# Feed-forward blocks of a four-layer trunk: one of the two left-hand tiles that share a buffer starts 192 bytes later

## The chip, the cores and the metric

The kernel is written for Trainium2 and runs on one core of one chip. The metric is the time of one execution on the device in microseconds (us), and of several runs the median is compared. The engines are named as in the profile: PE is TensorE's matmul side and PEld its weight loads, DVE is VectorE, ACT ScalarE, POOL GpSimd, SP SyncE. SBUF is the on-chip memory with 128 partitions; a tile takes the same bytes of each partition, and an address below is a byte within a partition.

## The reference

A trunk of four layers over 512 rows of width 1024. Each layer adds a mixer (S5, gated linear attention (GLA), differential attention, S5 again) and then a feed-forward part:

```
def swiglu_ffn(h, w_gate_up, w_down):
    g, u = jnp.split(h @ w_gate_up, 2, axis=-1)
    return (jax.nn.silu(g) * u) @ w_down

for layer in range(DEPTH):
    h = rmsnorm(x, norm_mix[layer])
    ...
    x = x + mix.astype(x.dtype)
    h = rmsnorm(x, norm_ffn[layer])
    x = x + swiglu_ffn(h, ffn_w_gate_up[layer], ffn_w_down[layer]).astype(x.dtype)
return rmsnorm(x, norm_final)
```

The hidden width is 2816, and all data are 32-bit floats.

## The kernel before, in words

**Split numbers.** A 32-bit product is made of three matmuls in the float32r type. Each operand is kept as a high and a low part: ACT writes the high part (a cast, line 366 for weights), DVE the difference to it (line 374). The matmuls are high by high, high by low, low by high. A weight tile's pair is `whl`, of which there are five buffers of 8,192 bytes each.

**Blocks of the feed-forward part.** The hidden width is cut into 11 blocks of 256. A block's gate and up products are not eight products of quarters but seven, by a Strassen-like scheme: sums of quarters of the left side are multiplied by sums of quarters of the weights. `seven_product` (line 561) issues one such product as 24 matmuls: two halves `j` of the output, four pieces `k` of the inner width, three pairs of high and low. In each of them the weights (128x128, from `whl`) are the stationary operand and the left side (128x256) is the moving one. PE loads the weights of a matmul while an earlier one streams. From a block's number 2 on the order within the block is one, five, six, two, seven, three, four, so `one` is the first product and `two` the fourth. `one` accumulates into the bank `a`, `two` into the bank `d`. The names of their left sides are "11" and "12", and both lie in one tile, `sides`. The other five products take their left sides from tiles of their own: `side1` (five), `side2` (six), `side3` (seven), `side4` (three) and `side22` (four), in the profile all `side`. The first two blocks of each layer are interleaved by a written list of steps (`plan` in `ffn`); there the two `two` follow each other, then `five` and `six` of both, while ACT and DVE make the left sides `side1`, `side2` and so on, and the weights.

After each three or four blocks, `gemm_b` multiplies their results (`act`) with the down weights (lines 394 to 396, 512 columns at a time), and its last pieces write x.

**Who orders the work.** Within an engine the written order stands. Tiles come from pools with a fixed number of buffers; a pool's buffers lie side by side, and pools lie in the order in which they are opened: constants (`cp`), x (`xp`), left sides (`hp`, tag hT, two buffers), weights (`wp`), norms (`np_`), small statistics (`sp`), and behind them what each stage opens. So a pool that grows moves all that lies behind it. `Sides.room` takes the two buffers of tag hT for the tile of the four quarters (`halves`, F in the code) and for `sides`. `edge` takes some bytes only so that what follows begins later.

The start addresses, as the program is built, and what is left of them after division by 512:

| tile | start, before | rest | start, after | rest |
|---|---|---|---|---|
| `whl`, five buffers, 8,192 apart | 63,424 | 448 | 63,936 | 448 |
| "11", high part (in `sides`) | 30,656 or 47,040 | 448 | 30,144 or 47,040 | 448 |
| "12", high part (in `sides`) | 38,848 or 55,232 | 448 | 38,528 or 55,424 | 128 |
| `side1`, `side2` | 132,736, 140,928 | 128 | the same | 128 |
| `side4`, `side3`, `side22`, layers 1 and 2 | 149,120 and on | 128 | the same | 128 |
| `side4`, `side3`, `side22`, layers 0 and 3 | 194,432 and on | 384 | the same | 384 |
| `act` | 149,184 and on | 192 | the same | 192 |

A part's four pieces `k` lie 1,024 bytes apart, the low part of a left side and of a weight pair 4,096 behind its high part, and the second half `j` of a weight piece 512 behind the first. So the rest by 512 is the same for all 24 matmuls of a product.

**The small tiles.** `cos2` and `sin2` are the tables of the rotation in the attention layer; `diff_tables` writes them during layer 1's feed-forward part, `factors` reads them once. `pw` holds powers for the S5 layers and was last read in layer 0's feed-forward part. `ms` in GLA's `readout`, `st`, `sums` and `nm` in the attention are statistics from the pool `sp`, with eight buffers each where nothing else is said.

Of the kernel before, what the change touches and what calls it, by code (L numbers as in the profile page):

```python
# [11 lines left out]
F32 = mybir.dt.float32  # L12
F32R = mybir.dt.float32r
# [3 lines left out]
ALU = mybir.AluOpType  # L17
# [4 lines left out]
P = 128  # L22
# [45 lines left out]
class Left:  # L68
# [18 lines left out]
    def room(self):  # L87
        self.hT = [self.tr.hp.tile([P, KT, SEQ], F32R, tag="hT", name=f"hT{z}") for z in range(2)]
# [72 lines left out]
class Sides(Left):  # L161
# [11 lines left out]
        return xs  # L173

    def room(self):
        F = self.tr.hp.tile([P, 4, 4, 256], F32, tag="hT", name="halves")
        self.whole = F
        self.F = {(0, 0): F[:, 0], (1, 0): F[:, 1], (0, 1): F[:, 2], (1, 1): F[:, 3]}
        two = self.tr.hp.tile([P, 2, 2, 4, 256], F32R, tag="hT", name="sides")
        self.place = {"11": two[:, 0], "12": two[:, 1]}  # L180
        self.heads = []

    def quarter(self, q, half, b):
# [9 lines left out]
    def open(self, pool, names):  # L193

        for n in names:
            self.place[n] = pool.tile([P, 2, 4, 256], F32R, name="side" + n)

    def freed(self):

        return [self.F[k] for k in ((0, 0), (0, 1), (1, 0), (1, 1))]  # L200

    def parts(self, name, src, ks=slice(0, 4)):
        o = self.place[name][:, :, ks]
        self.tr.nc.scalar.copy(o[:, 0], src)
        self.tr.nc.vector.tensor_tensor(o[:, 1], src, o[:, 0].bitcast(F32), op=ALU.subtract)

    def keep(self, t, d, p):
        for j in range(4):
# [24 lines left out]

    def high(self, name):
        for ks, y in self.of(name):
            self.tr.nc.scalar.copy(self.place[name][:, 0, ks], y)

    def low(self, name):
        for ks, y in self.of(name):
            o = self.place[name][:, :, ks]  # L240
            self.tr.nc.vector.tensor_tensor(o[:, 1], y, o[:, 0].bitcast(F32), op=ALU.subtract)


class Chunks:
# [42 lines left out]
class Trunk:  # L287
# [263 lines left out]
    def seven_product(self, side, w, bank, first, hl=None):  # L551

        if hl is None:
            hl = self.halves(w, 4, 256)
        mm = self.nc.tensor.matmul
        for j in range(2):
            c = slice(j * P, (j + 1) * P)
            o = bank[:, j * 256 : (j + 1) * 256]
            for k in range(4):
                for n, (x, y) in enumerate(((0, 0), (0, 1), (1, 0))):  # L560
                    mm(  # L561
                        o, hl[:, x, k, c], side[:, y, k], start=first and not (j or k or n),
                        stop=k == 3 and n == 2, skip_group_check=True,
                    )

# [1287 lines left out]
    def gla(self, l, left):  # L1853
# [5 lines left out]
        with self.tc.tile_pool(name="gla", bufs=1) as p:  # L1859
# [112 lines left out]
            def readout(hf, t):  # L1972
                st, o_h = sts[hf], on[hf]
                oo = row(self.tp("op"))
                ms = self.sp.tile([P, 2], F32, tag="ms2", name="ms")
                for z in range(2):
                    h = 2 * hf + z
                    zs = slice(z * 256, (z + 1) * 256)
                    for c in range(2):
                        ch = 2 * t + c  # L1980
                        nc.tensor.matmul(
                            oo[c * 64 : (c + 1) * 64, zs], qT[:, h, ch * 64 : (ch + 1) * 64], st[z][:, ch],
                            start=True, stop=True,
                        )
                for z in range(2):
                    junk = T("e")
                    nc.scalar.activation(
                        junk[:, :256], oo[:, z * 256 : (z + 1) * 256], AF.Square, scale=1.0 / 16.0,
                        accum_out=ms[:, z : z + 1],
                    )  # L1990
                r_ = self.rsqrt(ms[:], 2, 1e-6)
                for z in range(2):
                    h = 2 * hf + z
                    zs = slice(z * 256, (z + 1) * 256)
                    v.scalar_tensor_tensor(
                        o_h[:, t, zs], oo[:, zs], r_[:, z : z + 1], ng[:, h * 256 : (h + 1) * 256],
                        op0=ALU.mult, op1=ALU.mult,
                    )
# [67 lines left out]
    def diff_tables(self):  # L2066
        nc, i = self.nc, self.i
        v = nc.vector
        cp = self.cp
        self.cos2 = cp.tile([P, NT, 16], F32, name="cos2")  # L2070
        self.sin2 = cp.tile([P, NT, 16], F32, name="sin2")
        self.cidq = cp.tile([P, NT], F32, name="cidq")
        self.neglam = cp.tile([P, 1], F32, name="neglam")
        yield
        p = Slices(self.wp.tile([P, 2048], F32, tag="whl", name="dtab", bufs=5))
        if True:
            pi = p.tile([NT, P], I32, name="pi")
            nc.sync.dma_start(pi[:], i["positions"][0].rearrange("(t p) -> t p", p=P))
            ci = p.tile([NT, P], I32, name="ci")
            v.tensor_scalar(ci[:], pi[:], 6, None, op0=ALU.arith_shift_right)  # L2080
            pf = p.tile([NT, 2, P], F32, name="pf")
            v.tensor_copy(pf[:, 0], pi[:])
            v.tensor_copy(pf[:, 1], ci[:])
            yield
            yield
            yield
            ps = self.tp("pps")
            for z in range(2):
                nc.tensor.transpose(ps[:, z, :NT], pf[:, z], self.ident[:NT, :NT])
            yield  # L2090
            yield
            pos = p.tile([P, NT], F32, name="pos")
            v.tensor_copy(pos[:], ps[:, 0, :NT])
            v.tensor_copy(self.cidq[:], ps[:, 1, :NT])
            ang = p.tile([P, NT, 8], F32, name="ang")
            freq = np.float32(500000.0) ** (-np.arange(8, dtype=np.float32) / np.float32(8))
            for j in range(8):
                v.tensor_scalar_mul(ang[:, :, j], pos[:], float(freq[j]))
            yield
            red = p.tile([P, 32], F32, name="red")  # L2100
            self.reduce_angle(p, red[:], ang[:].rearrange("p t j -> p (t j)"), 32, "r")
            sn = p.tile([P, NT, 8], F32, name="sn")
            cs = p.tile([P, NT, 8], F32, name="cs")
            fl = lambda x: x[:].rearrange("p t j -> p (t j)")
            yield
            self.sincos(p, fl(sn), fl(cs), red[:], 32, "r")
            yield
            yield
            for z in range(2):
                v.tensor_copy(self.cos2[:, :, z * 8 : z * 8 + 8], cs[:])  # L2110
            v.tensor_scalar_mul(self.sin2[:, :, 0:8], sn[:], -1.0)
            v.tensor_copy(self.sin2[:, :, 8:16], sn[:])
            yield
            lm = p.tile([P, 4, 64], F32, name="lm")
            for z, s in enumerate(("diff_lam_q1", "diff_lam_k1", "diff_lam_q2", "diff_lam_k2")):
                nc.sync.dma_start(lm[:, z], i[s][0].partition_broadcast(P))
            pr = p.tile([P, 2, 64], F32, name="pr")
            lv = lm[:].rearrange("p (a b) n -> p a b n", b=2)
            v.tensor_tensor(pr[:], lv[:, :, 0], lv[:, :, 1], op=ALU.mult)
            sm = p.tile([P, 2], F32, name="sm")  # L2120
            v.tensor_reduce(sm[:], pr[:], op=ALU.add, axis=AX.X)
            ex = p.tile([P, 2], F32, name="ex")
            yield
            self.exp(p, ex[:], sm[:], 2, "l")
            yield
            v.tensor_tensor(self.neglam[:], ex[:, 1:2], ex[:, 0:1], op=ALU.subtract)
            v.tensor_scalar_add(self.neglam[:], self.neglam[:], -LAMBDA_INIT)

    def diff(self, l, left):
# [4 lines left out]
        with self.tc.tile_pool(name="diff", bufs=1) as p:  # L2134
# [90 lines left out]
            def prepare(j):  # L2225
# [13 lines left out]
                        self.nc.gpsimd.dma_start(qs[to, m], hl[rows, z, 0])  # L2239
                        self.nc.gpsimd.dma_start(ks[to, m], hl[rows, :, 1])  # L2240
                ready[j] = qs, ks
                st = self.sp.tile([P, 2, NT], F32, tag="st", name="st")
                o_s = p.tile([P, NT, P], F32, tag="o_s", name="o_s", bufs=2)
                kept[j] = st, o_s

# [2 lines left out]
            def scores(i):  # L2248
# [1 line left out]
                ts = slice(t * P, (t + 1) * P)  # L2250
                qs, ks = ready[j]
                st = kept[j][0]
                pr, sums = [], self.sp.tile([P, 4], F32, tag="sums", name="sums")
                ss = [self.sbank("s"), self.sbank("s")]
                for m in range(2):
                    for z in range(2):
                        nc.tensor.matmul(ss[m][:], qs[:, m, ts], ks[:, m, z], start=z == 0, stop=z == 1)  # L2257
                for m in range(2):
                    e = T("pr", 4)
                    nm = self.sp.tile([P, 1], F32, tag="nm", name="nm")  # L2260
                    v.tensor_tensor_reduce(  # L2261
                        e[:], ss[m][:], mask[:, t], -0.125, 3e38, op0=ALU.add, op1=ALU.min, accum_out=nm[:]
                    )
                    sum_ = st[:, 0, t : t + 1] if m == 0 else sums[:, 1:2]
                    nc.scalar.activation(e[:], e[:], AF.Exp, scale=-1.0, bias=nm[:], accum_out=sum_)  # L2265
                    pr.append(e)
# [209 lines left out]
```

## Time and profile before

| what | value |
|---|---|
| median of 3 runs | 2307.91 us (2306.17 to 2310.44) |
| profiled execution, own time | 2306.32 us |
| its span, first to last instruction | 2304.6 us |
| mean granted TensorE clock | 0.988 |
| PE, PEld busy | 96%, 85% of the span |
| DVE, ACT, POOL busy | 68%, 49%, 12% |

A row of a group gives line, engine, operation, output and inputs, shapes and count, then the busy time and the mean of one in ns, then the idle time ahead of them and what ended it. Matmuls overlap, so the mean of one (its latency) is longer than the step from one start to the next. A row of the timeline gives the start and length of a merged stretch; the step between two stretches is the difference of their starts.

### The profile page before, as it was taken

To read this page: it belongs to the slowest core of one execution; us is meant where nothing else is said; L and a number is where in the kernel's file an instruction comes from. 1 tells how busy PE (TensorE), PEld (TensorE's weight loads), DVE (VectorE), ACT (ScalarE), POOL (GpSimd) and SP (SyncE) were. 2 spreads that over 40 slices of the span, in tenths; PEclk is the share of its full clock that TensorE was granted. 3 is DMA by queue.
4 is the path that set the end of the run, shared out by engine and by line. 5 is a ranking of instruction groups with operands and counts; after the bars stand their busy time and mean duration, and the time that the engine had idled before them with its cause. 6 is when DMAs were issued, how large, how long until landed. Compare 5 with 4: busy or idle time off the path is not lost. (4 is left out here: it accounts for less than half of the span.)

```text
span 2304.6 us, 37230 instructions
## 1 busy us (share of the span) xinstructions
PE 2218.9 (96%) x14847; PEld 1967.2 (85%) x14847; DVE 1569.8 (68%) x2430; ACT 1120.4 (49%) x1865; POOL 280.3 (12%) x386
## 2 busy tenths in 40 slices
PE   5889999999999999999999999999999899999997
PEld 3778979898877799998987787999999788989996
DVE  7873887776624469777745675876766964967674
ACT  5634645454452456555535675744534224635342
POOL 1000140512000010101002131111000100101000
PEclk8999999999999999999999999999999899999999
DMA  4246666664422457766337365886641546767521
GB/s 86 40 111 187 142 179 167 173 170 110 120 74 73 130 140 191 188 160 174 92 115 154 89 147 148 212 224 144 167 100 46 144 143 162 178 170 171 155 78 64
DMA packets 295319, 317.83 MB, mean 138 GB/s; under 512 B 72205, under 2 KB 235337, under 8 KB 294890
## 3 DMA queue, kind: packets, MB, share of 16 engines
q1 hardware_dynamic: 232906, 234.23, 34.1%
q0 software_dynamic: 62240, 81.22, 19.1%
q8 instruction: 117, 1.92, 0.4%
q14 instruction: 56, 0.46, 0.1%
HBM read 283.54 MB, written 16.65 MB: 130 GB/s over the span
## 5 line engine op out<-in xcount | busy, mean ns | idle before, releaser
L374 DVE TENSOR_TENSOR whl<-wst,whl 128x1024 fp32r<-128x1024 f32 x272 | 331.4, 1222 | 255.7 <-ACT whl L366 254.7
L366 ACT CAST whl<-wst 128x1024 fp32r<-128x1024 f32 x272 | 284.0, 1050 | 316.4 <-PE acc L396 227.8
L561 PE MATMUL a<-side,whl 128*128 128x256 f32 x3168 | 382.9, 277 | 4.0 <-DVE whl L374 3.0
L561 PEld LDWEIGHTS a<-side,whl 128*128 128x128 f32 x3168 | 370.3, 188 | 6.3 <-DVE whl L374 4.1
L394 PE MATMUL acc<-whl,act 128*128 128x512 f32 x704 | 278.3, 396 | 1.4 <-DVE x L544 1.4
L396 PE MATMUL acc<-whl,act 128*128 128x512 f32 x704 | 274.7, 390 | 0.0
L395 PE MATMUL acc<-whl,act 128*128 128x512 f32 x704 | 274.6, 390 | 0.0
L561 PE MATMUL c<-side,whl 128*128 128x256 f32 x2112 | 254.0, 277 | 1.2 <-DVE whl L374 1.2
L561 PEld LDWEIGHTS c<-side,whl 128*128 128x128 f32 x2112 | 246.6, 188 | 1.8 <-DVE whl L374 1.8
L374 DVE TENSOR_TENSOR whl<-slot,whl 128x1024 fp32r<-128x1024 f32 x107 | 130.5, 1222 | 70.1 <-ACT whl L366 70.1
L394 PEld LDWEIGHTS acc<-whl,act 128*128 128x128 f32 x704 | 132.1, 188 | 31.7 <-issue 2.7
L396 PEld LDWEIGHTS acc<-whl,act 128*128 128x128 f32 x704 | 132.1, 188 | 28.1
L395 PEld LDWEIGHTS acc<-whl,act 128*128 128x128 f32 x704 | 132.2, 188 | 25.6
L366 ACT CAST whl<-slot 128x1024 fp32r<-128x1024 f32 x107 | 112.2, 1053 | 85.1 <-PE acc L396 35.2
L394 PE MATMUL acc<-whl,hT 128*128 128x512 f32 x352 | 143.0, 406 | 2.5 <-DVE ro L2203 1.5
L395 PE MATMUL acc<-whl,hT 128*128 128x512 f32 x352 | 138.0, 392 | 0.9 <-DVE whl L374 0.9
L396 PE MATMUL acc<-whl,hT 128*128 128x512 f32 x352 | 138.0, 392 | 0.0
L561 PE MATMUL a<-sides,whl 128*128 128x256 f32 x1056 | 134.4, 283 | 0.0
L561 PE MATMUL d<-sides,whl 128*128 128x256 f32 x1056 | 132.8, 282 | 1.0 <-ACT whl L366 1.0
L561 PEld LDWEIGHTS a<-sides,whl 128*128 128x128 f32 x1056 | 129.7, 191 | 1.1
L561 PEld LDWEIGHTS d<-sides,whl 128*128 128x128 f32 x1056 | 128.7, 191 | 1.2 <-ACT whl L366 1.2
L700 ACT CAST act<-r 128x512 fp32r<-128x512 f32 (+1 forms) x110 | 66.3, 645 | 114.1 <-DVE r L679 107.6
(452 smaller groups left out, 3892.3 us busy)
## 6 DMA issues: line engine op xcount, KB each, us to landing
wst<-in_ffn_w_gate_up_dram SPq DMA_DIRECT2D x88, 512.0 KB, 4.6
wst<-in_ffn_w_down_dram SPq DMA_DIRECT2D x88, 512.0 KB, 4.4
slot<-in_ffn_w_gate_up_dram SPq DMA_DIRECT2D x71, 512.0 KB, 5.5
wst<-in_ffn_w_gate_up_dram POOLq DMA_DIRECT2D x44, 512.0 KB, 6.3
halves<-in_ffn_w_gate_up_dram SPq DMA_DIRECT2D x43, 512.0 KB, 5.1
wst<-in_s_w_glu_dram SPq DMA_DIRECT2D x32, 512.0 KB, 4.6
wst<-in_gla_w_in_dram SPq DMA_DIRECT2D x24, 512.0 KB, 3.7
wst<-in_diff_w_qkv_dram SPq DMA_DIRECT2D x24, 512.0 KB, 3.9
```

Source lines behind the costliest of these rows:

```text
L366: self.last["high"] = self.nc.scalar.copy(hl[:, 0], w[:])
L374: self.last["low"] = self.nc.vector.tensor_tensor(hl[:, 1], w[:], hl[:, 0].bitcast(F32), op=ALU.subtract)
L394: mm(out, lh, rh, start=first, stop=False)
L395: mm(out, lh, rl, start=False, stop=False)
L396: self.last["mm"] = mm(out, ll, rh, start=False, stop=last)
L561: mm(o, hl[:, x, k, c], side[:, y, k], start=first and not (j or k or n), stop=k == 3 and n == 2, skip_group_check=True,)
L700: self.last["act high"] = nc.scalar.copy(dst[:, 0, j], src[:, j])
```

## The change

- `sides` becomes a flat tile of 4,224 floats, 128 more than before. "11" stays at its beginning, and "12" begins at float 2,096 in place of 2,048, which is 48 floats or 192 bytes later. High and low parts of one side still lie 4,096 bytes apart. `sides` is taken ahead of `halves`, so the two swap buffers.
- Both buffers of tag hT grow by 512 bytes. `cos2` and `sin2` lose their tiles and take the first 128 floats of `pw`; x and the lower buffer of tag hT then begin 512 bytes earlier, and the weights, the norms and the first statistics 512 bytes later.
- `ms`, `st`, `sums` and `nm` go from eight buffers to four, and so all that the stages open begins where it did.

```
     def room(self):
+        two = self.tr.hp.tile([P, 4224], F32R, tag="hT", name="sides")
         F = self.tr.hp.tile([P, 4, 4, 256], F32, tag="hT", name="halves")
         ...
-        two = self.tr.hp.tile([P, 2, 2, 4, 256], F32R, tag="hT", name="sides")
-        self.place = {"11": two[:, 0], "12": two[:, 1]}
+        at = lambda n: two[:, n : n + 1024].rearrange("p (k n) -> p k n", k=4)
+        self.place = {"11": (at(0), at(1024)), "12": (at(2096), at(3120))}
...
     def parts(self, name, src, ks=slice(0, 4)):
-        o = self.place[name][:, :, ks]
-        self.tr.nc.scalar.copy(o[:, 0], src)
-        self.tr.nc.vector.tensor_tensor(o[:, 1], src, o[:, 0].bitcast(F32), op=ALU.subtract)
+        hi, lo = (y[:, ks] for y in self.place[name])
+        self.tr.nc.scalar.copy(hi, src)
+        self.tr.nc.vector.tensor_tensor(lo, src, hi.bitcast(F32), op=ALU.subtract)
...
                     mm(
-                        o, hl[:, x, k, c], side[:, y, k], start=first and not (j or k or n),
+                        o, hl[:, x, k, c], side[y][:, k], start=first and not (j or k or n),
...
-                ms = self.sp.tile([P, 2], F32, tag="ms2", name="ms")
+                ms = self.sp.tile([P, 2], F32, tag="ms2", name="ms", bufs=4)
...
-        self.cos2 = cp.tile([P, NT, 16], F32, name="cos2")
-        self.sin2 = cp.tile([P, NT, 16], F32, name="sin2")
+        flat = self.pw[:].rearrange("p z n s -> p (z n s)")
+        self.cos2, self.sin2 = (flat[:, z * 64 : z * 64 + 64].rearrange("p (t j) -> p t j", t=NT) for z in range(2))
...
-                st = self.sp.tile([P, 2, NT], F32, tag="st", name="st")
+                st = self.sp.tile([P, 2, NT], F32, tag="st", name="st", bufs=4)
...
-                pr, sums = [], self.sp.tile([P, 4], F32, tag="sums", name="sums")
+                pr, sums = [], self.sp.tile([P, 4], F32, tag="sums", name="sums", bufs=4)
...
-                    nm = self.sp.tile([P, 1], F32, tag="nm", name="nm")
+                    nm = self.sp.tile([P, 1], F32, tag="nm", name="nm", bufs=4)
```

`open`, `high` and `low` of the left sides change as `parts` does: a side is now a pair of parts in place of one tile.

No instruction is added, removed or moved on any engine: each runs the same operations on the same shapes in the same order. The only waits that differ are on ACT in GLA, in `readout`, whose squares (`e,ms<-op`) write the statistics `ms`. This is ACT's row of work there before; `op` is the bank that is read out, `wst` a loaded weight tile.

```order
L1987 ACTIVATE e,ms<-op 128x256 [waits PE_49,Activation_49]
L1987 ACTIVATE e,ms<-op 128x256 [waits Activation_49]
L366 CAST whl<-wst 128x1024 [waits DMAHW6_49,DVE_49,PE_49]
L1987 ACTIVATE e,ms<-op 128x256 [waits PE_49,Activation_49]
L1987 ACTIVATE e,ms<-op 128x256 [waits Activation_49]
L366 CAST whl<-wst 128x1024 [waits DMAHW7_49,DVE_49,PE_49]
L1987 ACTIVATE e,ms<-op 128x256 [waits PE_49,Activation_49]
```

And this is the same place of the changed program on ACT, with lines two higher.

```order
L1989 ACTIVATE e,ms<-op 128x256 [waits PE_49,Activation_49]
L1989 ACTIVATE e,ms<-op 128x256 [waits Activation_49]
L368 CAST whl<-wst 128x1024 [waits DMAHW6_49,DVE_49,PE_49]
L1989 ACTIVATE e,ms<-op 128x256 [waits PE_49,Activation_49,Pool_49]
L1989 ACTIVATE e,ms<-op 128x256 [waits Activation_49]
L368 CAST whl<-wst 128x1024 [waits DMAHW7_49,PE_49]
L1989 ACTIVATE e,ms<-op 128x256 [waits PE_49,Activation_49,Pool_49]
```

Nothing moved; from the fifth of the eight readouts on, the first square also waits for POOL, which raises to a power the statistics of the readout four before.

More of the change, by code (lines that the diff above doesn't have):

```diff
@@ L195, in open @@
         for n in names:
-            self.place[n] = pool.tile([P, 2, 4, 256], F32R, name="side" + n)
+            y = pool.tile([P, 2, 4, 256], F32R, name="side" + n)
+            self.place[n] = (y[:, 0], y[:, 1])
     def freed(self):
@@ L235, in high @@
         for ks, y in self.of(name):
-            self.tr.nc.scalar.copy(self.place[name][:, 0, ks], y)
+            self.tr.nc.scalar.copy(self.place[name][0][:, ks], y)
     def low(self, name):
         for ks, y in self.of(name):
-            o = self.place[name][:, :, ks]
-            self.tr.nc.vector.tensor_tensor(o[:, 1], y, o[:, 0].bitcast(F32), op=ALU.subtract)
+            hi, lo = (z[:, ks] for z in self.place[name])
+            self.tr.nc.vector.tensor_tensor(lo, y, hi.bitcast(F32), op=ALU.subtract)
 class Chunks:
```

## The prediction

> **What bounds the kernel now.** I read the page's engine rows first, then the groups by line, then the timeline of one steady block, then the chain of waits.
>
> ```profile
> span 2304.6 us, 37230 instructions
> PE 2218.9 (96%) x14847; PEld 1967.2 (85%) x14847; DVE 1569.8 (68%) x2430; ACT 1120.4 (49%) x1865; POOL 280.3 (12%) x386
> L561 PE MATMUL a<-side,whl 128*128 128x256 f32 x3168 | 382.9, 277 | 4.0 <-DVE whl L374 3.0
> L561 PE MATMUL c<-side,whl 128*128 128x256 f32 x2112 | 254.0, 277 | 1.2 <-DVE whl L374 1.2
> L561 PE MATMUL a<-sides,whl 128*128 128x256 f32 x1056 | 134.4, 283 | 0.0
> L561 PE MATMUL d<-sides,whl 128*128 128x256 f32 x1056 | 132.8, 282 | 1.0 <-ACT whl L366 1.0
> L561 PEld LDWEIGHTS a<-side,whl 128*128 128x128 f32 x3168 | 370.3, 188 | 6.3 <-DVE whl L374 4.1 <-ACT whl L366 1.3 <-ACT r L607 0.7
> L561 PEld LDWEIGHTS d<-sides,whl 128*128 128x128 f32 x1056 | 128.7, 191 | 1.2 <-ACT whl L366 1.2
> ```
>
> PE is busy for 96% of the span, and the seven products wait almost nowhere (the last column), so what shortens a matmul there shortens the run, as long as DVE, ACT and the loads keep up. The same instruction has two speeds. The two products that read `sides` take 283 and 282 ns a matmul, the five that read a `side` 277. Their weight loads take 191 against 188. `sides` is also the one left side whose start leaves the same rest by 512 as the weights (448 and 448); the others leave 128 or 384.
>
> The timeline of PE for one steady block (start, length, stretch) gives the steps. The order is one, five, six, two, seven, three, four, then the down product:
>
> ```profile
> 1112.53 3.02 PE L561 MATMUL a<-sides,whl 128*128 128x256 f32 x24
> 1115.39 2.90 PE L561 MATMUL c<-side,whl 128*128 128x256 f32 x24
> 1118.13 2.88 PE L561 MATMUL a<-side,whl 128*128 128x256 f32 x24
> 1120.85 3.02 PE L561 MATMUL d<-sides,whl 128*128 128x256 f32 x24
> 1123.71 2.90 PE L561 MATMUL a<-side,whl 128*128 128x256 f32 x24
> 1126.45 2.88 PE L561 MATMUL c<-side,whl 128*128 128x256 f32 x24
> 1129.17 2.88 PE L561 MATMUL a<-side,whl 128*128 128x256 f32 x24
> 1131.89 0.39 PE L394 MATMUL acc<-whl,act 128*128 128x512 f32 x1
> ```
>
> From start to start `two` (bank d) takes 1123.71 - 1120.85 = 2.86 us, six 2.72, three 2.72, four 2.72. Each product that follows one on `sides`, five and seven, takes 2.74: 0.02 more, as if the loads had first to catch up. Over 24 matmuls that is 119 ns a step against 113.
>
> **The change part by part.** *The fourth product.* "12" gets the rest 128, exactly that of `side1` and `side2`, with the weights at 448 as before and the same distances between pieces and parts. If the rest decides, `two` falls from 2.86 to 2.72 us and the following product from 2.74 to 2.72: 0.16 us a block, 44 blocks, 7.0 us. "11" stays at 448, so `one` keeps its 2.86. That sets the most that can be had; now what of it lands.
>
> In 36 of the 44 blocks (number 2 to 10 of each layer) the products run back to back as above. Their cover is this:
>
> ```profile
> 1104.35:1123.71 19.36, 19.36 (x170) 19.36 (x169) 16.24 (x19) 11.24 (x14) 0.00 (x0) 1.00 0.17 55
> ```
>
> The columns of this window (one whole block) are length, busy time of PE, PEld, DVE, ACT and POOL, clock, share of the DMA engines, GB/s. DVE, the next busiest, has 3.1 us to spare in 19.36, and the DMA engines are 17% busy; 0.16 us less for PE does not use that up. So 36 x 0.16 = 5.76 us land, but for layer 2's first two of these blocks. There the chain of waits and PE's timeline show
>
> ```profile
> 1507.17 10.28 DMA wst<-in_ffn_w_gate_up_dram
> 1525.34 2.88 PE L561 MATMUL c<-side,whl 128*128 128x256 f32 x24
> 1528.74 3.06 PE L561 MATMUL a<-side,whl 128*128 128x256 f32 x24 [0.52 <-ACT r L607]
> ```
>
> PE stands 0.52 us behind work that began with a late load; what `two` gains ahead of that (2 x 0.16 = 0.32) is waited away. That leaves 5.44.
>
> In the first two blocks of a layer, the two `two` follow each other. The chain of waits has them as one stretch of 48, and then PE's timeline and DVE's are
>
> ```profile
> 1960.93 5.76 PE d L561 x48
> 1971.98 3.11 PE L561 MATMUL a<-side,whl 128*128 128x256 f32 x24
> 1970.95 1.23 DVE L374 TENSOR_TENSOR whl<-lent,whl 128x1024 fp32r<-128x1024 f32 x1 [0.52 <-ACT whl L366]
> ```
>
> The `six` at 1971.98 takes 3.11 where the steady one took 2.88. Its third matmul needs the low part that DVE finishes at 1970.95 + 1.23 = 1972.18, some 0.2 us after `six` began: DVE, which waits for ACT there and not for PE, sets the pace. With `two` 0.32 us shorter per layer, `six` would only stand longer. I take nothing for these 8 blocks, and 4 x 0.32 = 1.28 as the upper end.
>
> *The low end of the main term.* The nearest row for the new place is `side1`'s and `side2`'s, with the same rest and the same weights. The other end is `sides` itself, gain zero. I take the former, since all five tiles with rest 128 or 384 run at one speed.
>
> *All else that moves by 512 bytes.* Weights, x, the norms and one buffer of tag hT move by whole multiples of 512, and no rest by 512 changes there. Halves `j` 512 apart, pieces 1,024 apart and parts 4,096 apart already make up each 2.72 us product, and none of these distances shows in it. Zero.
>
> *The swapped buffers and `sides` first.* `sides` and `halves` change places; the waits of PE, DVE, POOL and SP are what they were. Zero. The writes into "12" keep their shape. Zero.
>
> *Tables in `pw`.* Four small DVE writes and two reads go to other bytes. The last reader of `pw` is long done by then, on the same engine:
>
> ```profile
> L1098 DVE TENSOR_TENSOR halves<-halves,pw x32: 347/388/428, 310.0 to 528.9; 128x256 f32<-128x256 f32 x16, 128x192 f32<-128x192 f32 x16
> L2111 DVE TENSOR_SCALAR sin<-dtab x1: 178/178/178, 917.2 to 917.2; 128x32 f32<-128x32 f32 x1
> ```
>
> Between 528.9 and 917.2 us nothing is near. Zero.
>
> *Four buffers for statistics.* ACT's added wait in GLA is for POOL's power of four readouts before:
>
> ```profile
> 705.03 0.69 POOL L485 TENSOR_TENSOR rs<-ms,mhalf 128x2 f32<-128x2 f32 x1 [90.28 <-DVE ms L483]
> 734.67 0.38 ACT L1987 ACTIVATE e<-op 128x256 f32<-128x256 f32 x1
> L1987 ACTq EVENT_SEMAPHORE  x6: 17/17/17, 711.4 to 752.4; - x6
> ```
>
> The first power ends at 705.72, and the fifth readout's square begins at 734.67, 29 us later; what is queued behind it on ACT, weight casts, is not held. Should each of the four waits cost what ACT's semaphore instructions take there, 17 ns, that is 0.07 us. `st`, `sums` and `nm` add no wait. Zero.
>
> **Sum.** 5.44 us. Against the profiled execution's own time that is 2306.32 - 5.44 = 2300.9; the median of the runs lies 1.6 above that execution, and from it 2307.91 - 5.4 = 2302.5 us. Between zero and 7.0 + 0.1 lie the bounds.
>
> [...]
>
> **The rivals.**
>
> *The address is not the cause (2307.9).* `sides` differs from the others in two more ways: it is in the lower part of SBUF, on the same side as the weights, and its starts differ from theirs. A move by 192 bytes would change nothing. For it speaks that equal rests cost nothing elsewhere:
>
> ```profile
> L1470 PE MATMUL y<-out,prods 128*128 128x128 f32 x256 | 36.8, 290 | 2.9 <-DVE prods L1461 2.9
> L1470 PE MATMUL y<-scr,prods 128*128 128x128 f32 x256 | 36.7, 291 | 0.0
> L396 PE MATMUL acc<-whl,act 128*128 128x512 f32 x704 | 274.7, 390 | 0.0
> L396 PE MATMUL acc<-whl,hT 128*128 128x512 f32 x352 | 138.0, 392 | 0.0
> ```
>
> `scr` and `hT` leave the rest 448 against 448, `out` and `act` do not, and the rows differ by 1 to 2 ns. But line 1470 is not float32r, and at 512 columns a weight load has twice the time to hide; neither is the case of `two`. The place in the lower half holds for `scr` and `hT` too, so they speak against it as much. Chance 0.15.
>
> *Given back later (2305).* Something other than PE paces more of the 36 blocks than layer 2's first two, and half the gain or more is waited away. The idle column of the products (4.0, 1.2 and 1.0 us in all) speaks against it. Chance 0.10.
>
> *Slower (2334 at the worst).* The weights move 512 bytes against the tiles that stay where they were, `side1` to `side22`. If places repeat at more than 512, these products, now fast, could fall to the slow step: 3168 + 2112 = 5280 matmuls by 119 - 113 = 6 ns is 32 us, less 5.4. It needs one in six of them to turn the sign. Against it stands that the 24 matmuls of a product already go through shifts of 512, 1,024 and 4,096 at one speed. Chance 0.05.
>
> **How the numbers follow.** The gain lands as summed: 0.70; not the address: 0.15; given back: 0.10; slower: 0.05. About 0.2%, 4.6 us, is what a measurement of this kernel can tell from no change. The runs before spread over 4.3 us, so a gain of 5.4 is measured as more than 4.6 in some 85% of its cases: 0.70 x 0.85 = 0.60, and a few of the given-back cases make it 0.62 for faster. Within 0.2%: the rest of these, the unchanged case and most of the given-back one, 0.32. Slower by more: the slower case and a little spread of the unchanged one, 0.06. The range runs from all 44 blocks landing and a low median (2307.9 - 7.1 - 1.5 = 2299.3) to the given-back case with some spread, 2306.5; outside it lie the unchanged case and the slower one, near 0.2.
>
> **What the changed profile would show.** If right: the row d<-sides at 277 ns and 128 us busy with weight loads at 188, a<-sides still at 283 and 134; in a steady block, `two` 2.72 and seven 2.72 from start to start, `one` 2.86; the `six` of a layer's first block longer by up to 0.3; PE some 6 us less busy; line 1470 and lines 394 to 396 as they are. If d<-sides stays at 282, the cause is not the rest by 512. If d falls and the span doesn't, look for PE's idle time ahead of the products. Rows of `side` above 277 would be the slower case.

## The result, and the profile after

The changed kernel takes 2303.32 us in the median of 22 runs (2295.57 to 2305.80), the kernel before 2308.54 us in 22 runs beside them (2302.79 to 2313.81). The ratio is 0.9976 with a 95% interval of 0.9969 to 0.9984: 5.2 us faster, forecast 5.4. The profiled execution took 2300.71 us (before 2306.32) at a mean granted clock of 0.987 (before 0.988).

These are the rows of the page and of the groups by line that answer to those of before; lines of code stand two higher, so L563 is the old L561. The one instruction more is a semaphore wait of ACT in GLA.

```profile
span 2298.6 us, 37231 instructions
PE 2212.9 (96%) x14847; PEld 1961.5 (85%) x14847; DVE 1566.1 (68%) x2430; ACT 1119.9 (49%) x1865; POOL 280.4 (12%) x386
L563 PE MATMUL a<-side,whl 128*128 128x256 f32 x3168 | 382.4, 277 | 3.9 <-DVE whl L376 3.6
L563 PE MATMUL c<-side,whl 128*128 128x256 f32 x2112 | 254.5, 277 | 1.2 <-DVE whl L376 1.2
L563 PE MATMUL a<-sides,whl 128*128 128x256 f32 x1056 | 134.5, 283 | 0.0
L563 PE MATMUL d<-sides,whl 128*128 128x256 f32 x1056 | 126.5, 276 | 1.0 <-ACT whl L368 1.0
L563 PEld LDWEIGHTS d<-sides,whl 128*128 128x128 f32 x1056 | 122.8, 188 | 1.2 <-ACT whl L368 1.2
```

One group moved: bank `d`, which is `two`, from 282 to 276 ns and from 132.8 to 126.5 us, its loads from 191 to 188 ns. Bank `a` of `sides`, which is `one`, and all `side` rows stand still. PE is busy 6.0 us less, and the span is 6.0 us shorter. The timeline of PE for the block that was shown of before:

```profile
1111.13 3.02 PE L563 MATMUL a<-sides,whl 128*128 128x256 f32 x24
1113.99 2.90 PE L563 MATMUL c<-side,whl 128*128 128x256 f32 x24
1116.73 2.88 PE L563 MATMUL a<-side,whl 128*128 128x256 f32 x24
1119.45 2.88 PE L563 MATMUL d<-sides,whl 128*128 128x256 f32 x24
1122.17 2.88 PE L563 MATMUL a<-side,whl 128*128 128x256 f32 x24
...
1130.33 0.39 PE L396 MATMUL acc<-whl,act 128*128 128x512 f32 x1
```

From start to start `one` takes 2.86 us, five 2.74, `two` 2.72 and seven 2.72. The block takes 1130.33 - 1111.13 = 19.20 us where it took 1131.89 - 1112.53 = 19.36: the 0.16 forecast.

Most of what the two `two` at the head of a layer gained was waited away. In layer 3 they take 5.46 us from their first start to the next product's (5.76 before), and the next rows show PE's timeline from the first `six` on, of before and then of after:

```profile
1971.98 3.11 PE L561 MATMUL a<-side,whl 128*128 128x256 f32 x24
1974.93 1.05 PE L154 MATMUL rows<-diag,ones 128*128 128x128 f32 x8
```

```profile
1967.16 0.39 PE L563 MATMUL a<-side,whl 128*128 128x256 f32 x2
1967.74 2.79 PE L563 MATMUL a<-side,whl 128*128 128x256 f32 x22 [0.19 <-DVE whl L376]
1970.36 1.05 PE L154 MATMUL rows<-diag,ones 128*128 128x128 f32 x8
```

The `six` takes 3.20 us from its start to the next (before 2.95), and stops after two matmuls for the low part that DVE writes. Of the 0.32 us gained there 0.25 come back as waiting.

Some terms of the difference are not the change's. These are windows of one stretch of GLA, of before and then of after (length, busy time of PE, PEld, DVE, ACT and POOL with counts, granted clock, share of the DMA engines, GB/s):

```profile
655.00:690.00 35.00, 35.00 (x158) 28.08 (x157) 10.18 (x11) 15.56 (x20) 0.00 (x0) 0.95 0.30 87
```

```profile
655.00:690.00 35.00, 35.00 (x151) 28.03 (x150) 9.59 (x10) 13.92 (x19) 0.00 (x0) 0.90 0.30 87
```

PE does seven matmuls less there, at a lower granted clock, and by the starts of its matmuls loses 1.6 us of its lead. The granted clock is 0.50 for 6.8 us there, where it was 0.50 for 3.4 us before, and half of the difference is 1.7 us. In S5's first stage the matmuls of line 1472 on `scr` rise from 291 to 305 ns in the same way: 59 of 256 have about twice the usual step where 34 had it before, and the median step is 112 ns in both. Over the whole run such stretches come out even: 0.988 against 0.987. In GLA the stretch at 0.50 begins at 672.2 us in the trace of before and at 669.9 in that of after; what sets its start and its length no run here shows.

### The profile page after: what moved, and what is told of

The parts are those of the page before. It is cut to its first block, busy times and chain, and to the rows that moved or that the text cites. A ratio compares the mean times of both kernels' runs of the same rounds, so it can differ in the third digit from the quotient of the medians.

```text
span 2298.6 us, 37231 instructions
## 1 busy us (share of the span) xinstructions
PE 2212.9 (96%) x14847; PEld 1961.5 (85%) x14847; DVE 1566.1 (68%) x2430; ACT 1119.9 (49%) x1865; POOL 280.4 (12%) x386
## 5 line engine op out<-in xcount | busy, mean ns | idle before, releaser
L563 PE MATMUL a<-side,whl 128*128 128x256 f32 x3168 | 382.4, 277 | 3.9 <-DVE whl L376 3.6
L563 PEld LDWEIGHTS a<-side,whl 128*128 128x128 f32 x3168 | 369.1, 188 | 6.7 <-DVE whl L376 5.4
L563 PE MATMUL c<-side,whl 128*128 128x256 f32 x2112 | 254.5, 277 | 1.2 <-DVE whl L376 1.2
L563 PEld LDWEIGHTS c<-side,whl 128*128 128x128 f32 x2112 | 246.8, 188 | 2.0 <-DVE whl L376 2.0
L563 PE MATMUL a<-sides,whl 128*128 128x256 f32 x1056 | 134.5, 283 | 0.0
L563 PEld LDWEIGHTS a<-sides,whl 128*128 128x128 f32 x1056 | 129.7, 191 | 1.2
L563 PE MATMUL d<-sides,whl 128*128 128x256 f32 x1056 | 126.5, 276 | 1.0 <-ACT whl L368 1.0
L563 PEld LDWEIGHTS d<-sides,whl 128*128 128x128 f32 x1056 | 122.8, 188 | 1.2 <-ACT whl L368 1.2
```

Of the source, the lines that this page charges most:

```text
L563: mm(o, hl[:, x, k, c], side[y][:, k], start=first and not (j or k or n), stop=k == 3 and n == 2, skip_group_check=True,)
```

## The experiments

All kernels start from the changed kernel where nothing else is said, and all comparisons are with the kernel before, run on the same chip. "Distance" below is the start of the left side less the start of the weights, in bytes, after division by 256; why 256 the third experiment shows. `sides` had distance 0 before the change, all `side` tiles 192, and "12" has 192 after it. In the seven products that is the moving operand less the stationary one. In the down product and the other `acc` matmuls of 512 columns the parts are exchanged: `act` (or `hT`, `zT`, `oT`) is stationary and the weights stream, so there the moving operand less the stationary one is 256 less the distance.

**Everything but the 192 bytes.**

```
-        self.place = {"11": (at(0), at(1024)), "12": (at(2096), at(3120))}
+        self.place = {"11": (at(0), at(1024)), "12": (at(2048), at(3072))}
```

> The changed kernel with the 192 bytes taken back: "12" starts at float 2,048 of the flat tile, as "11" at 0, so both leave the rest 448 like the weights; the swapped buffers, the tables in pw and the four statistics buffers stay. If the equal rest is the cause: d<-sides 282 to 283 ns a matmul, `two` 2.86 us in a steady block, seven 2.74, and the time of before (2308, ratio 0.998 to 1.002). If the rest of the change made the gain: some 2303, ratio near 0.9976.

Measured: 2308.00 us (12 runs), ratio 1.0003 (0.9994 to 1.0012). The group of `two` is back:

```profile
L563 PE MATMUL d<-sides,whl 128*128 128x256 f32 x1056 | 132.8, 282 | 1.0 <-ACT whl L368 1.0
```

So tables in `pw`, four buffers, swapped buffers and the 512-byte moves are together worth nothing that can be told (by the interval at most some 3 us), and the gain is the 192 bytes'.

**"11" moved as well.**

```
-        self.place = {"11": (at(0), at(1024)), ...
+        self.place = {"11": (at(48), at(1072)), ...
```

> The changed kernel with "11" moved by the same 192 bytes (floats 48 and 1,072), so no left side has the rest of the weights. If the equal rest is the cause: a<-sides falls from 283 to 277 ns as d did, `one` from 2.86 to 2.72 us and five from 2.74 to 2.72, 0.16 us in each of 36 steady blocks less layer 2's first two (34 x 0.16 = 5.4) below the changed kernel: about 2298, ratio to before 0.995 to 0.996. If something else of `one` holds it (it comes right behind the down product, and its weights are made ahead): a<-sides stays at 283 and the time near 2303.

Measured: 2317.46 us (5 runs), ratio 1.0042 (1.0030 to 1.0054): slower than before, where a second gain was expected. PE's timeline of layer 0, at the end of one block and in a later one, behind a down product:

```profile
501.86 2.88 PE L563 MATMUL c<-side,whl 128*128 128x256 f32 x24
504.58 2.88 PE L563 MATMUL a<-side,whl 128*128 128x256 f32 x24
507.30 0.39 PE L396 MATMUL acc<-whl,act 128*128 128x512 f32 x1
...
547.68 2.99 PE L563 MATMUL a<-sides,whl 128*128 128x256 f32 x24
550.51 2.99 PE L563 MATMUL c<-side,whl 128*128 128x256 f32 x24
553.34 2.99 PE L563 MATMUL a<-side,whl 128*128 128x256 f32 x24
```

All seven left sides now have distance 192, and yet a product takes either 2.72 us (113.3 ns a step) or 2.83 us (117.8 ns). The pace holds from product to product and block to block, and in this run changes only behind a down product or a stall. In this profile 171 products ran at the slow one, in all layers; 171 x 0.107 = 18 us, more than moving both saves. Of products without a stall inside the changed kernel had one at that pace, the kernel before none.

**The weights moved instead.** On the kernel before, with only the tables put in `pw`: the weights begin 192 bytes later, and 320 more restore what lies behind them. All left sides stay.

```
+        self.edge(self.wp, 192)
+        self.edge(self.sp, 320)
```

> The kernel before with no left side moved in its rest; instead all weight pairs begin 192 bytes later (rest 128 in place of 448), paid with the tables in pw and 320 bytes behind the statistics. Left sides keep 448 (`sides`), 128 (side1, side2, and side3, side4, side22 of layers 1 and 2) and 384 (those three of layers 0 and 3). If the equal rest with the weights is the cause, the slow ones swap: sides 277 ns; side1 and side2 283 in all layers, side3, side4, side22 283 in layers 1 and 2 and 277 in layers 0 and 3. In time: layers 0 and 3 two slow products as before, layers 1 and 2 five in place of two, 3 x 0.14 x 18 steady blocks = 7.6 us more, ratio about 1.003. If it lies in the tile `sides` or in its place in the lower part of SBUF: sides stays at 283, side at 277, time as before.

Measured: 2352.40 us (5 runs), ratio 1.0194 (1.0180 to 1.0209), far more than expected. Groups by line and one block on PE's timeline:

```profile
L563 PE MATMUL a<-side,whl 128*128 128x256 f32 x3168 | 402.1, 283 | 3.2 <-DVE whl L376 3.0
L563 PE MATMUL c<-side,whl 128*128 128x256 f32 x2112 | 266.5, 283 | 0.0
L563 PE MATMUL d<-sides,whl 128*128 128x256 f32 x1056 | 130.8, 279 | 0.1
L398 PE MATMUL acc<-whl,act 128*128 128x512 f32 x704 | 278.6, 396 | 0.0
```

```profile
1118.87 3.04 PE L563 MATMUL c<-side,whl 128*128 128x256 f32 x24
1121.75 3.04 PE L563 MATMUL a<-side,whl 128*128 128x256 f32 x24
1124.63 2.99 PE L563 MATMUL d<-sides,whl 128*128 128x256 f32 x24
1127.46 3.04 PE L563 MATMUL a<-side,whl 128*128 128x256 f32 x24
```

The slow group has swapped: the five `side` products, whose tiles did not move, now take 2.88 us each, and the two on `sides`, at distance 64, 2.83. So it is the distance to the weights that decides, not the place of `sides`. The runs at other distances below bear it out: there the weights stay and a left side goes to distance 64, and its product takes 2.83 us too. Two things were not expected. In layers 0 and 3 `side4`, `side3` and `side22` have the rest 384 by 512 against the weights' 128 and are as slow as those with equal rests: the period is 256 bytes, not 512. And the matmuls of 512 columns slowed too, from 390 to 396 ns; from start to start the step goes from 227 to some 233 ns. By 256 those on `acc` all had distance 0 before and have 64 here, which is 192 for the moving operand less the stationary one. Of the 46.1 us between this profile's span (2350.7) and that of before, 24 lie in the seven products and 20 in the 512-column matmuls of the down product, of S5 and of the projections (10.6, 4.5 and 5.1), by differences of their starts.

**Other distances, one run each.** `sides` at another pair of distances in each layer (`a` and `b` count floats of four bytes).

```
...
+        a, b = ((4, 8), (16, 24), (32, 64), (40, 96))[self.l]
+        self.place = {"11": (at(a), at(1024 + a)), "12": (at(2048 + b), at(3072 + b))}
```

> The changed kernel with another start of each left side of `sides` in each layer, in bytes behind the rest of the weights, "11" and "12": layer 0 16 and 32, layer 1 64 and 96, layer 2 128 and 256, layer 3 160 and 384. Read by the step of the 24 matmuls, 2.86 us slow and 2.72 fast. If only an equal rest by 512 is slow, all eight are 2.72. If a smaller distance repeats (64, 128 or 256 bytes), those that are a multiple of it are 2.86. If it needs a least distance, 16 and 32 are between. If the address has no part in it, all stay at 2.86.

```
...
+        a, b = ((12, 20), (28, 36), (44, 52), (56, 60))[self.l]
```

> Eight more distances between left side and weights, one of "11" and one of "12" in each layer, in bytes: layer 0 48 and 80, layer 1 112 and 144, layer 2 176 and 208, layer 3 224 and 240. The distances so far gave by steady product: 0 and 256 2.86 to 2.88 us, 16 to 160 and 384 2.80 to 2.87, 64 (weights moved) 2.83, 192 and 448 2.72 or 2.83. If the period is 256 bytes and 192 is the only place with a fast pace: 2.80 or more at all eight. If what counts is only that the left side's start is 16 bytes or more ahead of or behind the weights: some of 176 to 240 reach 2.72.

Measured: 2310.92 and 2310.68 us. The time of a steady product from start to start, by distance:

| distance | us | distance | us |
|---|---|---|---|
| 0 | 2.86 to 2.88 | 128 | 2.85 to 2.88 |
| 16 | 2.80 to 2.85 | 144, 176 | 2.86 |
| 32 | 2.80 | 160 | 2.81 to 2.86 |
| 48, 80 | 2.84 | 192 | 2.72 or 2.83 |
| 64 | 2.83 | 208 | 2.86 |
| 96 | 2.87 | 224 | 2.83 |
| 112 | 2.76 | 240 | 2.81 |

Of the sixteen, only 192 was seen at 2.72, and one more, 112, comes near it. "Any unequal rest is fast" is wrong; the change hit the one good distance of the table.

The same two runs show that the pace at 192 also depends on the product ahead, without any stall or down product between. This is PE's timeline of the second one in layer 1, with `one` at distance 112 and `two` at 144:

```profile
1119.78 2.92 PE L565 MATMUL a<-sides,whl 128*128 128x256 f32 x24
1122.54 2.89 PE L565 MATMUL c<-side,whl 128*128 128x256 f32 x24
...
1127.98 3.02 PE L565 MATMUL d<-sides,whl 128*128 128x256 f32 x24
1130.84 2.99 PE L565 MATMUL a<-side,whl 128*128 128x256 f32 x24
1133.66 2.99 PE L565 MATMUL c<-side,whl 128*128 128x256 f32 x24
```

Behind `one`, five takes 2.72 us; behind `two`, seven takes 2.82, and so it is in all nine of the layer's later blocks. Behind 16 all eight products without a stall are slow too; behind 80 and 240 all ten are fast; behind 128 and 160 both occur.

**`one` moved in place of `two`.** "11" at distance 192, "12" at 0.

```
+        self.place = {"11": (at(48), at(1072)), "12": (at(2176), at(3200))}
```

> The changed kernel with the two sides' parts exchanged: "11" at the distance 192 (floats 48 and 1,072), "12" at an equal rest with the weights (floats 2,176 and 3,200). Theory of two paces: at the distance 192 the stream of matmuls can run at 113 or at 118 ns a step, keeps the pace it has, and a product at an equal rest leaves the fast one behind it. Then `two` takes 2.86 us and seven, three, four behind it 2.72 always, and one, five, six of the next block 2.72 too, but for the first block behind a down product, where they may take 2.83; time 2302 to 2307. Rival: one slow product a block is all that matters and which one is equal, no pace is kept: one 2.72, five 2.72 everywhere, 2303. Second rival: the pace is lost at each block's start: one, five and six 2.83 in all blocks, 3 x 0.107 x 36 = 11.5 us above the changed kernel, 2314.

Measured: 2307.32 us (12 runs), ratio 0.9993 (0.9981 to 1.0004): no gain that can be told. PE's timeline of a block behind a down product:

```profile
1074.66 2.99 PE L563 MATMUL a<-sides,whl 128*128 128x256 f32 x24
1077.49 2.99 PE L563 MATMUL c<-side,whl 128*128 128x256 f32 x24
1080.32 2.99 PE L563 MATMUL a<-side,whl 128*128 128x256 f32 x24
1083.14 3.04 PE L563 MATMUL d<-sides,whl 128*128 128x256 f32 x24
1086.02 2.90 PE L563 MATMUL a<-side,whl 128*128 128x256 f32 x24
1088.76 2.88 PE L563 MATMUL c<-side,whl 128*128 128x256 f32 x24
```

One, five and six take 2.83 us, `two` with its equal rest 2.88 here, and behind it the fast pace stands: 2.74, 2.72. 23 products in the profile run slow, all of them ahead of a `two`. A product at distance 0 is slow itself, but what follows it is fast (one exception stands below); here it comes fourth and covers less of the block than `one` does.

**A short head at equal rest.** Only the first of the four pieces of "11" stays at distance 0, the other three get 192; `Cut` returns piece 0 from one view and the rest from the other. Four instructions on ACT and four on DVE, in the whole kernel, are cut in two for it.

```
...
+        cut = lambda n: two[:, n : n + 768].rearrange("p (k n) -> p k n", k=3)
+        first = lambda n: two[:, n : n + 256].rearrange("p (k n) -> p k n", k=1)
+        self.place = {"11": (Cut(first(0), cut(560)), Cut(first(256), cut(1328))), "12": (at(2096), at(3120))}
```

> The changed kernel with "11" cut: its first piece k (6 of the 24 matmuls of `one`, three at the head of each half) keeps the equal rest, pieces 1 to 3 go to the distance 192. Its split takes two instructions each on ACT and DVE in place of one (four times in all, below 0.5 us each). Theory of two paces, if three matmuls at an equal rest are enough to leave the slow pace: one 2.75 to 2.79 us, all others 2.72, about 0.09 us a block or 3 us below the changed kernel: 2300. If three are too few: many products at 2.83, and a time between the changed kernel and the one with both moved, 2304 to 2317. If there were no kept pace: one 2.76 and 2300 as well, so it tells the first two apart.

Measured: 2299.64 us (10 runs), ratio 0.9962 (0.9951 to 0.9973), the lowest of all, though its interval still meets that of the changed kernel. One block on PE's timeline:

```profile
1108.64 2.92 PE L586 MATMUL a<-sides,whl 128*128 128x256 f32 x24
1111.40 2.88 PE L586 MATMUL c<-side,whl 128*128 128x256 f32 x24
1114.12 2.88 PE L586 MATMUL a<-side,whl 128*128 128x256 f32 x24
```

`one` takes 2.76 us, and everything behind it 2.72, but for four products at 2.83 behind a stall. So 6 of its 24 matmuls at distance 0 (the first piece of each half) are enough to leave the fast pace behind them.

**The down product's left side, one run each.** `act` at distances 192, 128, 64 and 32 in layers 0 to 3; and then, together with "11" moved as in the second experiment, at 192 in all layers.

```
-            self.edge(fp, 64)
+            s = (192, 128, 64, 32)[l]
+            self.edge(fp, 64 + s)
...
```

> The changed kernel with the down product's left side `act` moved as well: by 192, 128, 64 and 32 bytes in layers 0 to 3, so that it stands at these distances from its weights and no longer at 0 (by 256). Everything else stays. The run that moved the weights had its 512-column matmuls at distance 64 and at a step of 233 to 235 ns, where distance 0 has 227. Theory 'for 512 columns only the equal rest is at the floor': all four layers at 232 to 235 ns, 528 matmuls x 6.3 ns = 3.3 us a layer, 13 us in all, some 2316 us. Rival 'the distance that is good for 256 columns is good for 512 too': layer 0 at 227, the others slower, at most 10 us, 2305 to 2313. Rival 'the distance is not what slowed the 512 columns there': 227 in all layers, 2303.

> The run with both left sides at distance 192, and `act` at distance 192 as well in all layers, so that no product of a block and no down product has equal rests. Theory 'what the stream leaves behind decides the pace of the next one': the products behind a down product now all go at one pace, which may be either; with the slow one every product takes 2.83 us and the run some 2303 - 44 x 0.14 + 44 x 7 x 0.107 = 2330 us, with the fast one 2297, each plus up to 13 us if 512 columns at distance 192 take 233 ns. Rival 'it is chosen by chance at a stall': fast and slow blocks mixed as in that run, at other places, 2317 plus the same 13 at most.

Measured: 2316.43 us for the first (one run of the kernel before beside it: 2305.50). Two rows of its timeline, 18 matmuls apart, in layer 3:

```profile
2179.72 0.40 PE L398 MATMUL acc<-whl,act 128*128 128x512 f32 x1
...
2183.92 0.40 PE L398 MATMUL acc<-whl,act 128*128 128x512 f32 x1
```

(2183.92 - 2179.72) / 18 = 233.3 ns a step. The mean is 233 in layers 1 to 3, against 227 at distance 0. In layer 0 steps of 226, 229 and 232 ns follow each other in turn, 229 in the mean. The down products alone cost 10.4 us. Here `act` is the stationary operand, so the moving one less the stationary one is 64, 128, 192 and 224 bytes in layers 0 to 3. The distance that is good for 256 columns was thus tried in layer 2, not in layer 0, and it is slow at 512: 233.3 ns, and 233.4 in the run with the weights moved, which has it too. So of the five distances seen at 512 columns only the equal rest is at the floor, with 64 between it and the others.

This run also has the exception. Its `one` in layer 1 behind a down product is at distance 0, and all six products behind it are slow:

```profile
958.45 3.04 PE L563 MATMUL a<-sides,whl 128*128 128x256 f32 x24
961.33 2.99 PE L563 MATMUL c<-side,whl 128*128 128x256 f32 x24
964.16 2.99 PE L563 MATMUL a<-side,whl 128*128 128x256 f32 x24
```

The second took 2307.32 us (2305.50 beside it, one run each), with 42 slow products of 256 columns where the second experiment had 171, and again fast and slow groups of blocks. The theory of a single pace behind down products is wrong as it stands. But neither is it chance alone. Eight times a down product is followed by `one` at distance 192: with `act` at distance 0, seven of the eight are slow in the second experiment and the same seven in the one with `one` moved alone; with `act` moved, seven of the eight are fast. So what a down product leaves behind depends on its own distance, with an exception in each run. What makes the exceptions was not found.

## Why the prediction was right

*The fourth product.* Right: `two` 2.86 to 2.72, seven 2.74 to 2.72, 0.16 us a block. The first experiment gives all of the gain to the 192 bytes. The cause named, the rest by 512, was right only in part. What counts is the distance of left side and weights by 256, and 192 is not one of many good ones. The step held because it gave "12" exactly the rest of `side1` and `side2`; at another distance by 256 the table has 2.76 to 2.88 us for a product, and the forecast of 2.72 would have failed.

*36 blocks, less layer 2's first two.* The reduction by 0.32 us can't be told from chance. In that place of layer 2 the profile after shows

```profile
1524.01 2.88 PE L563 MATMUL c<-side,whl 128*128 128x256 f32 x24
1526.90 2.98 PE L563 MATMUL a<-side,whl 128*128 128x256 f32 x24
```

without the 0.52 us of waiting that stood there before: three takes 2.89 us to the next start, before 3.40. With the first experiment's layout, without a gain, it was 2.74, so that wait changes from run to run.

*The first two blocks of a layer at zero.* Nearly right, and seen in layer 3's `six`: from the first `two` to the first `one` of block 2 the four layers together got 0.3 us shorter, of 1.28 at most.

*All else at zero.* Right within what can be told: ratio 1.0003 for all of it without the 192 bytes.

*The sum.* 5.44 us against 5.2 measured, with an interval of 3.7 to 7.2.

*The rivals.* "The address is not the cause" fell with the first and third experiments. Its best row, equal speeds of `hT` and `act` in line 396, was no evidence either way: by 256 both have distance 0. (In the trace of before a weight load of that line takes 188 to 189 ns in a step of 227, one of the products 188 to 191 in a step of 113 to 120.) "Slower by the 512-byte move" fell with the first; a whole period of 256 can't show. A rival that the prediction didn't have is the slow pace at distance 192. It took one product here, because `one` at its equal rest opens each block. That was luck: with both sides moved it turned the sign, as the second experiment showed.

*Weights and moving side.* The place of the one against the other counts: with no instruction changed, moving either start by 192 bytes moves the step between 113, 118 and 120 ns. What the two streams share in the hardware no run here shows.

## What to carry to other kernels

For streams of 256-column float32r matmuls with a weight load each, look at the distance of the moving side's start from the weights' start by 256, and compare products of one kernel that differ in it before choosing; 192 was the good one here (113.3 ns a step, where 0 has 119 to 120), while for 512 columns distance 0 was (227 ns, where others have 229 to 233). Move one operand at a time and look at the products behind it, since a stream's pace can be set by what ran ahead of it: a slow product may be what keeps six others fast (2.86 us for `one` at distance 0 and 2.72 to 2.74 behind it, against 2.83 for all seven at 192 behind a down product). Where that is so, a short piece at the slow distance may do the same for less (2.76 us for `one` with six such matmuls of its 24).

## What the runs showed of the hardware that was not expected

- The step of a 256-column float32r matmul depends on the start of its moving operand less that of its stationary one, by 256 bytes: 113.3 ns at 192 in the better case, 119 to 120 at 0. At 512 columns it is 227 ns at 0, 229 at 64, and 233 at 128, 192 and 224.
- At 192 a stream of 256 columns has two stable paces, 113.3 and 117.8 ns, kept over blocks of 19 us. Which one it takes depends on what ran ahead: behind a product at distance 0 it was the fast one with one exception seen, behind 144 the slow one nine times of ten, behind a down product at distance 0 mostly the slow one. Six matmuls at distance 0 (0.7 us) lead back to the fast one. In the trace the weight load starts some 110 ns ahead of its matmul at the fast pace, 115 at the slow one, and 118 at distance 0.
- Line 1470 (now L1472), which isn't float32r and has 128 columns, has `scr` at distance 0 and `out` at 192 to `prods`, and a median step of 112 ns with both. So these two distances make no difference there; others were not tried.
